# Output projection of a hybrid decoder block by seven half-size products, with operand sums by accumulating transfers

## Chip, cores and metric

One core of one Trainium2 chip. The metric is the device time of one execution in microseconds; the kernel before has a median of 1336.53 us over 3 runs (1336.42 to 1337.27).

## What is computed

One decoder block on `x` of 1024 positions by 1024 columns, all in float32:

```python
h = rmsnorm(x, mix_norm_g)
p = h @ w_in                                   # q, k, v, latents, two gates g_a and g_b
A = sliding-window attention with sinks        # window 128
B = multi-head latent attention                # causal
y = sigmoid(g_a) * (A @ w_o_swa) + sigmoid(g_b) * (B @ w_o_mla)
x = x + y @ w_out                              # the output projection: 1024 x 1024 x 1024
x = x + (silu(h2 @ w_gate) * (h2 @ w_up)) @ w_down        # h2 = rmsnorm(x), the FFN
return rmsnorm(x, final_norm_g)
```

The change concerns `x + y @ w_out` and what stands around it.

## The kernel before

**Three passes for one float32 product.** An operand is split into a high part (a cast to fp32r on ACT, L163) and a low part (the difference, on DVE, L166): this pair is what `split` makes. `mm3` (L168 to L174) multiplies two split operands by three matmuls of 128x128 by 128x512 that add up in one PSUM bank: high by high (L172), high by low (L173), low by high (L174).

**Storage.** SBUF is cut into 21 slots `U` of 4 KB and 17 slots `V` of 8 KB for each partition; a tile waits until a slot is free. PSUM has two groups of four banks: `P1` (pool `ps1`) and `PX` (in this stage pool `psc`).

**The stages in order.** Input projections; sliding-window attention (about 132 to 315 us in the profile), in whose iterations the gate projections are made too; latent attention; then the mixing of the two attentions. In `mix_a` and `mix_b` each of eight column groups `dc` gets its two gates `ga`, `gb` (tiles `sg`), on which ACT applies the sigmoid (L1277). POOL multiplies the first attention's part (tile `ar`) into `ga` (L1442, two 128x512 instructions per group: the "gate products"). TensorE makes the second attention's part `oB`, DVE multiplies it by `gb` (L1428) and adds the two (L180): that is `y`, transposed, with 128 columns of `y` on the partitions and 1024 positions along them. It is split at once into four operand pairs (`yh`, `yl`), one for each half of columns and half of positions.

**The output projection.** `xo` is made in four segments (two halves of positions by two halves of output columns) of four blocks of 128 positions. Each block is 8 k-tiles x 3 passes = 24 matmuls into one `P1` bank, and DVE adds it to the block of `x` (L180, `x<-xo,x`). `w_out` is loaded in units of 512 KB on SP's queue and split just ahead of its use; the first column half is loaded and split twice, so there are 12 units.

**Towards the FFN.** When a block of `x` is complete, ACT squares it (L1652), POOL makes the reciprocal root (L311, L314: `ms`, `rstd`), DVE scales it (L1657, `xn`), and TensorE transposes it (`to_h`, L1483, eight transposes into two `PX` banks `tp`). The FFN's products already use seven half-size products instead of eight (class `Seven`), so `to_h` also makes sums of blocks: for positions 0 to 511 it keeps copies `hraw` and splits `b11` and `b21`; for 512 to 1023 it makes `t2`, `t3`, `b22` at once, and `hraw` becomes what `t1` and `t4` are split from later (`late_split`). What `to_h` returns (`lower`, `rest`) is the second half of this work, which the code places.

**What sets the order.** Ahead of the last segment of the projection a scheduler orders the instructions of each engine. From there on (`in_order`) TensorE, DVE, ACT and POOL run in the order in which the code is written, until the FFN is under way. Each engine works its queue strictly in order, and so do SP's queue of transfers and their waits.

## Time and profile before

| | |
|---|---|
| median of 3 runs | 1336.53 us |
| the profiled execution | 1336.93 us, of which the profile's span is 1335.1 us |
| TensorE busy | 1323.6 us (99%) |
| DVE, ACT, POOL busy | 904.6, 636.5, 567.0 us |
| the projection on TensorE | 603.9 to 696.3 us, the FFN from 697.1 us |
| transfers | 223.61 MB, mean 167 GB/s, nearly all started by SP |

Busy shares are means over the whole span; the stages differ. A row of the timeline gives the start, the duration, the engine, the line and what the instruction writes and reads; in brackets stands for how long the engine had been idle and what ended that.

### The profile page before, as it was taken

The page shows a single profiled execution, that of the slowest core. Times are in us where ns is not written, and L with a number is a line of the kernel's source. Part 1 is how long each engine was busy: PE and PEld are TensorE (multiplying, and loading weights), DVE is VectorE, ACT ScalarE, POOL GpSimd, SP SyncE. Part 2 cuts the span into 40 slices and gives each one's busy share as a digit, 9 for nine tenths or more (in the row PEclk, how much of TensorE's full clock was granted, in tenths as well). Part 3 has the DMA queues.
Part 4 walks back from the last instruction along what each step waited for, and adds up shares of the span by engine and source line. Part 5 has one row for each costly group of instructions (what it writes and reads, how often), then busy time and mean ns, then how long its engine had stood idle before and what let it go on. Part 6 is the DMA issues. An engine that isn't in the chain of part 4 may idle for free. (4 is left out here: it accounts for less than half of the span.)

```text
span 1335.1 us, 19045 instructions
## 1 busy us (share of the span) xinstructions
PE 1323.6 (99%) x6564; PEld 1115.3 (84%) x6564; DVE 904.6 (68%) x1471; ACT 636.5 (48%) x1291; POOL 567.0 (42%) x614
## 2 busy tenths in 40 slices
PE   9999999999999999999999999999999999999997
PEld 6899888888888889888887888888888888888886
DVE  7868777776767767696469766666665654664862
ACT  7434676675556766753335323322233233644443
POOL 2115556552325554451131765755666541022521
PEclk9999999999999999999999999999999999999999
DMA  9454322335575530681532354534443425996504
GB/s 376 154 188 163 108 104 83 119 115 193 160 246 151 111 95 17 252 291 56 222 129 91 143 182 172 200 133 181 181 162 142 169 95 191 386 381 223 174 16 142
DMA packets 85311, 223.61 MB, mean 167 GB/s; under 512 B 9632, under 2 KB 16288, under 8 KB 84128
## 3 DMA queue, kind: packets, MB, share of 16 engines
q1 hardware_dynamic: 83776, 220.05, 47.1%
q10 hardware_dynamic: 1440, 2.36, 0.5%
q8 instruction: 52, 0.85, 0.3%
q14 instruction: 43, 0.35, 0.1%
HBM read 151.72 MB, written 70.12 MB: 166 GB/s over the span
## 5 line engine op out<-in xcount | busy, mean ns | idle before, releaser
L166 DVE TENSOR_TENSOR wl<-wr,wl 128x512 fp32r<-128x512 f32 x150 | 148.7, 1015 | 71.2 <-ACT wl L163 70.9
L166 DVE TENSOR_TENSOR lrv<-lr,lrv 128x1024 fp32r<-128x1024 f32 x77 | 105.1, 1396 | 49.0 <-ACT lrv L163 46.4
L163 ACT CAST lrv<-lr 128x1024 fp32r<-128x1024 f32 x77 | 80.1, 1052 | 95.6 <-PE fd L174 69.5
L172 PE MATMUL fd<-lrv 128*128 128x512 f32 x308 | 119.8, 389 | 0.0
L173 PE MATMUL fd<-lrv 128*128 128x512 f32 x308 | 119.8, 389 | 0.0
L174 PE MATMUL fd<-lrv 128*128 128x512 f32 x308 | 119.8, 389 | 0.0
L177 POOL TENSOR_TENSOR wr<-wr,sm 128x512 f32<-128x512 f32 (+1 forms) x38 | 45.8, 1213 | 162.6 <-DVE wl L166 136.2
L163 ACT CAST wl<-wr 128x512 fp32r<-128x512 f32 x150 | 87.0, 623 | 1.4 <-DVE wr L835 1.1
L1206 POOL TENSOR_TENSOR denb<-denb,neg_one 128x1 f32<-128x1 f32 x64 | 40.1, 627 | 96.2 <-ACT p L1205 84.4
L166 DVE TENSOR_TENSOR wl<-sm,wl 128x512 fp32r<-128x512 f32 x60 | 48.2, 829 | 42.2 <-ACT wl L163 42.1
L173 PEld LDWEIGHTS fd<-lrv 128*128 128x128 f32 x308 | 57.8, 188 | 12.1
L174 PEld LDWEIGHTS fd<-lrv 128*128 128x128 f32 x308 | 57.8, 188 | 12.0
L172 PEld LDWEIGHTS fd<-lrv 128*128 128x128 f32 x308 | 57.8, 188 | 11.9
L311 POOL TENSOR_SCALAR ms<-ss 128x1 f32<-128x1 f32 x32 | 8.9, 277 | 138.0 <-ACT xn L1652 61.1
L1205 ACT ACTIVATE p<-scb,nmb 128x384 f32<-128x384 f32 (+3 forms) x64 | 47.8, 747 | 33.3 <-DVE nmb L1204 25.6
L166 DVE TENSOR_TENSOR ptl<-pTb,pth 128x512 fp32r<-128x512 f32 (+2 forms) x96 | 50.5, 551 | 16.6 <-ACT pth L163 16.2
L1204 DVE CUSTOM_DVE_ANT_0 scb<-scb,mask 128x384 f32<-128x384 f32 (+3 forms) x64 | 48.5, 760 | 15.0 <-PE scb L1196 13.0
L1537 ACT ACTIVATE act<-sm 128x512 f32<-128x512 f32 x11 | 7.0, 632 | 104.4 <-DVE sm L180 104.4
L1207 POOL TENSOR_SCALAR p<-p,denb 128x384 f32<-128x384 f32 (+3 forms) x64 | 48.0, 749 | 6.3
L1537 ACT ACTIVATE act<-pu 128x512 f32<-128x512 f32 x22 | 13.9, 633 | 70.6 <-DVE pu L180 70.6
L163 ACT CAST pth<-pTb 128x512 fp32r<-128x512 f32 (+2 forms) x96 | 43.5, 482 | 8.5 <-PE pTb L1221 7.5
L172 PE MATMUL fb<-t2h,wl 128*128 128x512 f32 x120 | 47.4, 395 | 0.0
(356 smaller groups left out, 4319.1 us busy)
## 6 DMA issues: line engine op xcount, KB each, us to landing
lr<-la_d SPq DMA_DIRECT2D x77, 256.0 KB, 5.4
wr<-in_w_gate_dram SPq DMA_DIRECT2D x22, 512.0 KB, 4.2
wr<-in_w_up_dram SPq DMA_DIRECT2D x22, 512.0 KB, 5.0
wd<-in_w_down_dram SPq DMA_DIRECT2D x22, 512.0 KB, 6.9
rb_d<-wd SPq DMA_DIRECT2D x22, 512.0 KB, 2.7
la_d<-sd SPq DMA_DIRECT2D x22, 512.0 KB, 5.7
lr<-rb_d SPq DMA_DIRECT2D x44, 256.0 KB, 5.4
lr<-in_w_down_dram SPq DMA_DIRECT2D x33, 256.0 KB, 5.4
```

Source lines behind the costliest of these rows:

```text
L163: i = nc.scalar.copy(hi, src)
L166: (eng or nc.vector).tensor_tensor(lo, src, hi.bitcast(F32), op=ALU.subtract)
L172: nc.tensor.matmul(ps, ah, bh, start=first and i == 0, stop=False, skip_group_check=go_on)
L173: nc.tensor.matmul(ps, ah, bl, start=False, stop=False, skip_group_check=go_on)
L174: nc.tensor.matmul(ps, al, bh, start=False, stop=last and i == n - 1, skip_group_check=go_on)
L177: eng.tensor_tensor(out, a, b, op=ALU.subtract)
L311: nc.gpsimd.tensor_scalar(ms, ss, 1.0 / width, EPS, op0=ALU.mult, op1=ALU.add)
L1204: nc.vector.tensor_tensor_reduce(s_, s_, m_, 1.0, -NEG, op0=ALU.add, op1=ALU.min, accum_out=nm)
L1205: nc.scalar.activation(p_, s_, AF.Exp, scale=-1.0, bias=nm, accum_out=den)
L1206: nc.gpsimd.tensor_tensor(den, den, neg_one[:, 0:1], op=ALU.pow)
L1207: nc.gpsimd.tensor_scalar(p[:, 0:w], p[:, 0:w], den, 0.0, op0=ALU.mult, op1=ALU.add)
L1537: nc.scalar.activation(dst, src, AF.Silu)
```

## The change

**The projection as seven products.** With `y` cut into quarters (columns 0 to 511: `a`, 512 to 1023: `b`, each with positions `lo` and `hi`; `b` is kept negated) and `w_out` into `b11`, `b12`, `b21`, `b22`, seven products numbered 1, 2, 5, 6, 3, 7, 4 replace the eight. Each has four blocks of 4 k-tiles x 3 passes, 48 matmuls. Products 1, 6, 7, 4 add up in one bank per block (group `PX`), 2, 5, 3 in another (`P1`), and after each product DVE adds the bank to a half of `x` or subtracts it. That makes 28 such instructions of 128x512, before 16.

**Sums of `w_out`.** Four sums `t1` to `t4` of 1 MB are made in DRAM (`wt_d`) during the sliding-window attention: SP copies, and POOL starts transfers that add the second term to what stands there (`out_sums`, in iterations 0 to 10). 14 units are loaded and split, before 12.

**Sums of `y`.** Products 1, 2 and 4 take quarters as they are; 12 of these splits are made while mixing, where 16 were. Products 5, 7, 6 and 3 take sums, which POOL makes in place by 16 accumulating transfers between SBUF tiles, 256 KB each (`left_sum`), four for each k. The second and third of a k need the first to have landed, the third needs the second, the fourth the third. 16 more splits follow (`split_left`).

**FFN.** The subtraction that made `hraw`'s second half on DVE (4 times, 128x512) becomes an accumulating transfer on POOL (`rest`), with the sign taken into the splits of `t4`. Transposes of blocks 0 to 3 use `P1` banks, those of blocks 4 to 7 the `PX` banks of products 4, so that block 4 takes those of `xo` blocks 0 and 1, block 5 those of blocks 2 and 3, and so on in turn.

**Order.** The whole projection is now in the order of the code; the column groups are mixed in the order 0, 1, 4, 5, 2, 3, 6, 7 (before 4, 5, 0, 1, 6, 7, 2, 3), and the halves that are spilled to DRAM and read back (`ar_d`) are those of groups 4 to 7. TensorE's order at the end of the projection is: product 3 block 3, 7 block 1, transposes 2, 4 block 0, 7 block 2, transposes 3, 4 block 1, 7 block 3, transposes 4, 4 block 2, 4 block 3, transposes 5, FFN product, transposes 6, FFN product, transposes 7.

```diff
-    OUT0 = (2, 0, 3, 1)
-    for r, hf in enumerate((0, 1, 0)):
-        for j in (range(4) if r else OUT0):
-            plain(("out", r, j), w_out[hf, j], (P, 2, 512), (r, j) != (2, 3))
+    for dp in (0, 2, 1, 3):
+        plain(("ob", dp), w_o_mla[dp], (P, 4, 256), True)
+    wt_d = [dram.tile([2, P, 2, 512], F32, name=f"wt_d{i}") for i in range(4)]
+    W_SRC = {1: w_out[0, 0:2], 2: w_out[0, 2:4], 3: w_out[1, 2:4], 5: wt_d[0], 6: wt_d[1], 7: wt_d[2], 4: wt_d[3]}
+
+    def out_unit(q, u):
+        def load():
+            raw = U("wr", F32, (P, 2, 512))
+            nc.sync.dma_start(raw, W_SRC[q][u])
+            return raw
+
+        def conv(raw):
+            hi, lo = halves_of((P, 2, 512), True)
+            if q == 6:
+                a = nc.scalar.activation(hi, raw, AF.Copy, scale=-1.0)
+                nc.vector.scalar_tensor_tensor(lo, raw, -1.0, hi.bitcast(F32), op0=ALU.mult, op1=ALU.subtract)
+            else:
+                split(hi, lo, raw)
+            return hi, lo
+
+        st.add(("out", q, u), load, conv)
+
+    for q in (1, 2, 5, 6, 3, 7, 4):
+        for u in range(2):
+            out_unit(q, u)
+
+    def more(dst, src, **kw):
+        nc.gpsimd.dma_start(dst, src, accum_op=ALU.add, **kw)
+
+    def rows(t):
+        return t.rearrange("j p k c -> (j p) (k c)")
+
+    def out_sums(i):
+        b11, b12, b21, b22 = (rows(w_out[hf, 2 * kh:2 * kh + 2]) for kh in range(2) for hf in range(2))
+        t1, t2, t3, t4 = (rows(t) for t in wt_d)
+        if i == 0:
+            nc.sync.dma_start(t1, b11)
+            nc.sync.dma_start(t3, b22)
+        if i == 2:
+            more(t1, b12, max_dma_last_dim=4096)
+            more(t3, b12, max_dma_last_dim=4096)
+        if i == 4:
+            nc.sync.dma_start(t2, t1)
+        if i == 6:
+            more(t2, b22, max_dma_last_dim=4096)
+        if i == 8:
+            nc.sync.dma_start(t4, t2)
+        if i == 10:
+            more(t4, b21, max_dma_last_dim=4096)
 
 
...
@@ -1035,6 +1078,7 @@
         if it + 1 < N_SW:
             sw_qT(it + 1)
         sw[it].pop("norm")()
+        out_sums(it - 1)
         gate_step()
         if it >= 1:
...
+    left = {}
+    ya = {}
+
+    def new_left(q):
+        left[q] = (V("yh", F32R), V("yl", F32R))
+
+        ya[dc] = ga
+
+        def mixed(sh):
+            cs = half(sh)
+            if dc < 4:
+                add(ga[:, cs], ga[:, cs], gb[:, cs], nc.vector)
+            else:
+                nc.vector.scalar_tensor_tensor(ga[:, cs], ga[:, cs], -1.0, gb[:, cs], op0=ALU.mult, op1=ALU.subtract)
+            if dc >= 4 or sh == 0:
+                hi, lo = left[1 if dc < 4 else 2 if sh == 0 else 4]
+                split(hi[:, dc % 4], lo[:, dc % 4], ga[:, cs])
+
         for sh in range(2):
             cs = half(sh)
             pb = PX("oB")
             mm3(pb, [((w[0][:, c, blk(dc % 2)], w[1][:, c, blk(dc % 2)]), obT[(c, sh)]) for c in range(4)])
             nc.vector.tensor_tensor(gb[:, cs], pb, gb[:, cs], op=ALU.mult)
             if i == 7:
-                add(ga[:, cs], ga[:, cs], gb[:, cs], nc.vector)
-                split(*hT(dc, cs), ga[:, cs])
+                mixed(sh)
         for sh in range(2 if i < 7 else 0):
-            cs = half(sh)
-            add(ga[:, cs], ga[:, cs], gb[:, cs], nc.vector)
-            split(*hT(dc, cs), ga[:, cs])
+            mixed(sh)
+    def left_sum(n, *ks):
+        for k in ks:
+            a_lo, a_hi, b_lo, b_hi = (ya[k + d][:, half(sh)] for d in (0, 4) for sh in range(2))
+            more(*{0: (b_hi, a_hi), 1: (a_hi, a_lo), 2: (a_lo, b_hi), 3: (b_lo, a_lo)}[n])
+
+    def split_left(q, *ks):
+        if q not in left:
+            new_left(q)
+        d, sh = {5: (4, 1), 7: (0, 1), 6: (0, 0), 3: (4, 0)}[q]
+        for k in ks:
+            split(left[q][0][:, k], left[q][1][:, k], ya[k + d][:, half(sh)])
...
+    new_left(1)
+    SUMS = {6: [(0, 0), (0, 1)], 7: [(0, 2), (1, 0), (1, 1)]}
+    pool_order = tc.manual_schedule(engines={engines.Pool})
+    pool_order.__enter__()
+    x2 = {}
+        for n, k in SUMS.get(i, ()):
+            left_sum(n, k)
+        if i == 2:
+            new_left(2)
+            new_left(4)
         mix_b(dc, i)
...
-            ps = PX("tp", (P, 4, P))
+            ps = (P1 if b < 4 else PX)("tp", (P, 4, P))
...
-                nc.scalar.copy(raw1[b][:, kh], pss[kh])
+                nc.scalar.activation(raw1[b][:, kh], pss[kh], AF.Copy, scale=1.0 - 2 * kh)
...
-        sub(r[:, 1], r[:, 1], t23[:, 0], nc.vector)
         def rest():
+            more(r[:, 1], t23[:, 0])
             sub(t23[:, 1], pss[1], t23[:, 1], nc.vector)
...
-            split_h(name, c, r[:, i])
+            if i == 0:
+                split_h(name, c, r[:, i])
+            else:
+                hi, lo = (t[:, :, blk(c)] for t in hq[name])
+                nc.scalar.activation(hi, r[:, i], AF.Copy, scale=-1.0)
+                nc.vector.scalar_tensor_tensor(lo, r[:, i], -1.0, hi.bitcast(F32), op0=ALU.mult, op1=ALU.subtract)
...
+    def xo(q, b):
+        if q in (1, 2, 5):
+            bank[("B" if q == 1 else "A", b)] = (PX if q == 1 else P1)("xo")
+        ps = bank[("B" if q in (1, 6, 7, 4) else "A", b)]
+        w = [st.get(("out", q, u)) for u in range(2)] if b == 0 else wop[q]
+        wop[q] = w
+        lh, ll = left[q]
+        mm3(ps, [((lh[:, k, blk(b)], ll[:, k, blk(b)]), (w[k // 2][0][:, k % 2], w[k // 2][1][:, k % 2]))
+                 for k in range(4)], first=q in (1, 2, 5), go_on=q in (6, 7, 4, 3))
+        x_ = x2[b if q in (1, 2, 6, 3) else 4 + b][:, lo if q in (1, 2, 4) else hi]
+        if q in (1, 5, 7):
+            add(x_, ps, x_, nc.vector)
+        else:
+            sub(x_, x_, ps, nc.vector)
+        if b == 3:
+            left.pop(q)
+            wop.pop(q)
...
+    def norm_a(b):
+        xn = U("xn")
+        ss = tiny("ss")
+        nc.scalar.activation(xn, x2[b], AF.Square, accum_out=ss)
+        normed[b] = xn, rstd_of(ss, D)
...
-    prev = None
-    for seg, (sh, hf) in enumerate(((0, 0), (0, 1), (1, 1), (1, 0))):
...
-            else:
-                ps = P1("xo")
-                mm3(ps, [(hT(k, blk(b)), (wo2[k // 2][0][:, k % 2], wo2[k // 2][1][:, k % 2])) for k in DCS])
-            add(x2[b][:, hs], ps, x2[b][:, hs], nc.vector)
...
+    in_order.__enter__()
+    for b in range(4):
+        x2[b] = load_x(b)
+    ahead(5, 1)
+    for n, k in ((0, 3), (1, 2), (2, 0), (2, 1), (1, 3), (2, 2), (3, 0), (3, 1), (2, 3), (3, 2), (3, 3)):
+        left_sum(n, k)
+    xo(1, 0)
+    conv(5, 0)
+    xo(1, 1)
+    conv(5, 1)
+    ahead(6, 1)
+    xo(1, 2)
+    split_left(5, 0, 1)
+    xo(1, 3)
+    split_left(5, 2)
+    xo(2, 0)
+    split_left(5, 3)
+    x2[4] = load_x(4)
+    x2[5] = load_x(5)
+    xo(2, 1)
+    conv(6, 0)
+    x2[6] = load_x(6)
+    x2[7] = load_x(7)
+    xo(2, 2)
+    conv(6, 1)
+    ahead(3, 1)
+    xo(2, 3)
+    split_left(6, 0, 1)
+    xo(5, 0)
+    conv(3, 0)
+    xo(5, 1)
+    split_left(6, 2, 3)
+    xo(5, 2)
+    conv(3, 1)
+    split_left(7, 0)
+    ahead(7, 1)
+    xo(5, 3)
+    split_left(3, 0, 1)
+    split_left(7, 1)
+    xo(6, 0)
+    split_left(3, 2, 3)
+    split_left(7, 2)
+    xo(6, 1)
+    conv(7, 0)
+    split_left(7, 3)
+    xo(3, 0)
+    norm_a(0)
+    conv(7, 1)
+    ahead(4, 1)
+    ffn.load_part(0, 0)
+    xo(6, 2)
+    norm_b(0)
+    ffn.load_part(0, 1)
+    xo(3, 1)
+    norm_a(1)
+    xo(6, 3)
+    norm_b(1)
+    to_h_of(0)
+    xo(3, 2)
+    norm_a(2)
+    conv(4, 0)
+    xo(7, 0)
+    norm_b(2)
+    to_h_of(1)
+    xo(3, 3)
+    norm_a(3)
+    conv(4, 1)
+    ffn.mix(0)
+    xo(7, 1)
+    norm_b(3)
+    to_h_of(2)
+    xo(4, 0)
+    norm_a(4)
+    ffn.prep_to(1)
+    xo(7, 2)
+    norm_b(4)
+    to_h_of(3)
+    xo(4, 1)
+    norm_a(5)
+    ffn.prep_to(2)
+    xo(7, 3)
+    norm_b(5)
+    to_h_of(4)
+    xo(4, 2)
+    norm_a(6)
+    ffn.prep_to(3)
+    xo(4, 3)
+    norm_b(6)
+    norm_a(7)
+    to_h_of(5)
+    for kh in range(2):
+        ffn.load_part(1, kh)
+    norm_b(7)
     ffn.n_ahead = 1
     ffn.run()
-    late_parts.pop(0)()
+    lowers.pop(4)()
+    ffn.prep_to(4)
+    to_h_of(6)
     ffn.run()
+    lowers.pop(5)()
     ffn.prep_to(5)
-    late_parts.pop(0)()
+    to_h_of(7)
     ffn.run()
     ffn.prep_to(6)
-    lower = to_h(*prev)
-    ffn.run()
+    lowers.pop(6)()
     ffn.run()
     ffn.prep_to(7)
-    lower()
+    ffn.run()
+    lowers.pop(7)()
     ffn.prep_to(8)
```

The first place is POOL's queue at the end of the mixing. Before: the last gate products (`sg<-ar,sg`), then the first block's reciprocal root.

```order
L1442 TENSOR_TENSOR sg_6821<-ar_6825,sg_6821 128x512 x2
L1442 TENSOR_TENSOR sg_6870<-ar_6874,sg_6870 128x512 x2
L311 TENSOR_SCALAR ms_7160<-ss_7158 128x1
L314 TENSOR_TENSOR rstd_7162<-ms_7160,neg_half 128x1
L311 TENSOR_SCALAR ms_7195<-ss_7193 128x1
```

After: behind the last gate products stand the accumulating transfers. `sg_6623`, `sg_6681`, `sg_6825`, `sg_6872` hold `y` of groups 4 to 7, `sg_6470`, `sg_6603`, `sg_6730`, `sg_6778` that of groups 0 to 3. The first row of them is sum (0, k = 0), the sixth is (0, k = 3).

```order
L1513 TENSOR_TENSOR sg_6825<-ar_6829,sg_6825 128x512 x2
L1513 TENSOR_TENSOR sg_6872<-ar_6876,sg_6872 128x512 x2
L328 DMA sg_6623<-sg_6470 128x512
L328 DMA sg_6681<-sg_6603 128x512
L328 DMA sg_6825<-sg_6730 128x512
L328 DMA sg_6470<-sg_6470 128x512
L328 DMA sg_6603<-sg_6603 128x512
L328 DMA sg_6872<-sg_6778 128x512
L328 DMA sg_6730<-sg_6730 128x512
L328 DMA sg_6470<-sg_6623 128x512
L328 DMA sg_6603<-sg_6681 128x512
L328 DMA sg_6778<-sg_6778 128x512
```

All sixteen transfers stand between the last gate product and the first root.

The second place is ACT's queue at the same time. Before: the two sigmoids of the last group (`sg_6870`, `sg_6872`) stand behind the first cast of the group before it (`sg_6821`).

```order
L163 CAST wv_6992<-wr_6868 128x1024
L163 CAST yh_6609<-sg_6821 128x512
L1277 ACTIVATE sg_6870<-sg_6870 128x1024
L1277 ACTIVATE sg_6872<-sg_6872 128x1024
L163 CAST yh_6611<-sg_6821 128x512
L163 CAST yh_6609<-sg_6870 128x512
```

After: those of the last group (`sg_6872`, `sg_6874`) stand ahead of all casts of the group before it (`sg_6825`).

```order
L163 CAST yh_6619<-sg_6778 128x512
L163 CAST wv_6997<-wr_6870 128x1024
L1321 ACTIVATE sg_6872<-sg_6872 128x1024
L1321 ACTIVATE sg_6874<-sg_6874 128x1024
L163 CAST yh_6738<-sg_6825 128x512
L163 CAST yh_6740<-sg_6825 128x512
L163 CAST yh_6738<-sg_6872 128x512
```

So the sigmoid for which the last gate product waits no longer stands behind a cast that waits for DVE's sum of that group.

The third place is where the projection ends and the FFN begins. DVE before, from `xn` of block 5 (`x<-xo,x` is the projection's evacuation, `hraw`, `t`, `t2l`, `b22l`, `t3l` are the work of `to_h` on transposes `tp`):

```order
L1657 SCALAR_TENSOR_TENSOR xn_7553<-x_7380,rstd_7558,ffng_6995 128x1024
L177 TENSOR_TENSOR t_1419_7576<-tp_7565,t_1419_7576 128x512
L177 TENSOR_TENSOR t2l_7573<-t_1419_7576,t2h_7572 128x4x128
L177 TENSOR_TENSOR b22l_7571<-tp_7565,b22h_7570 128x4x128
L177 TENSOR_TENSOR t3l_7575<-t_1419_7576,t3h_7574 128x4x128
L180 TENSOR_TENSOR x_7413<-xo_7590,x_7413 128x512
L177 TENSOR_TENSOR hraw_7265<-tp_7623,hraw_7265 128x512
L177 TENSOR_TENSOR t_1427_7633<-tp_7628,hraw_7265 128x512
L177 TENSOR_TENSOR hraw_7265<-hraw_7265,t_1427_7633 128x512
L1657 SCALAR_TENSOR_TENSOR xn_7616<-x_7413,rstd_7621,ffng_6995 128x1024
L166 TENSOR_TENSOR wl_7640<-wr_7328,wl_7640 128x512
L166 TENSOR_TENSOR wl_7643<-wr_7329,wl_7643 128x512
```

DVE after, from the evacuation of product 4, block 2 (`x_7139`), with the FFN operand's split `wl_7661` behind it and the evacuation of block 3 (`x_7141`) behind that:

```order
L177 TENSOR_TENSOR x_7139<-x_7139,xo_7066 128x512
L166 TENSOR_TENSOR wl_7661<-wr_7349,wl_7661 128x512
L177 TENSOR_TENSOR x_7141<-x_7141,xo_7086 128x512
L1733 SCALAR_TENSOR_TENSOR xn_7654<-x_7139,rstd_7659,ffng_7001 128x1024
L177 TENSOR_TENSOR hraw_7457<-tp_7686,hraw_7457 128x512
L177 TENSOR_TENSOR t_1436_7696<-tp_7691,hraw_7457 128x512
L1733 SCALAR_TENSOR_TENSOR xn_7679<-x_7141,rstd_7684,ffng_7001 128x1024
L177 TENSOR_TENSOR t_1424_7636<-tp_7625,t_1424_7636 128x512
L177 TENSOR_TENSOR t2l_7633<-t_1424_7636,t2h_7632 128x4x128
L177 TENSOR_TENSOR b22l_7631<-tp_7625,b22h_7630 128x4x128
L177 TENSOR_TENSOR t3l_7635<-t_1424_7636,t3h_7634 128x4x128
L166 TENSOR_TENSOR wl_7731<-wr_7350,wl_7731 128x512
```

ACT after, at the same place (`xn_7654` is the square of block 6, `wl_7661` the cast that the split on DVE waits for):

```order
L1579 COPY t_1424_7636<-tp_7620 128x512
L1581 CAST t2h_7632<-t_1424_7636 128x4x128
L1728 ACTIVATE xn_7654,ss_7655<-x_7139 128x1024
L163 CAST wl_7661<-wr_7349 128x512
L1728 ACTIVATE xn_7679,ss_7680<-x_7141 128x1024
L1579 COPY t_1436_7696<-tp_7686 128x512
L1581 CAST t2h_7632<-t_1436_7696 128x4x128
```

The evacuation of the last block now stands behind an FFN operand, and the lower parts of blocks 4 and 5 follow when both blocks' upper parts and two `xn` are done.

103 lines of the change are left out of this document (34 added, 69 removed).

## Prediction

> **What bounds the kernel now.** I read the page first, then the waits of TensorE, the groups that touch the output projection's result `xo`, and the timelines around it.
>
> ```profile
> PE 1323.6 (99%) x6564; PEld 1115.3 (84%) x6564; DVE 904.6 (68%) x1471; ACT 636.5 (48%) x1291; POOL 567.0 (42%) x614
> ```
>
> ```profile
> PE warm L510 <- DVE warm L507: 1.2, 1, 1.2
> PE scb L1194 <- ACT p L1205: 1.1, 3, 0.6
> ...
> PE fa L172 <- ACT wl L163: 0.4, 1, 0.4
> ```
>
> TensorE is busy for 1323.6 of 1335.1 us, and its longest single wait is 1.2 us. So a matmul taken away anywhere is worth its whole spacing, provided that nothing makes TensorE wait in its place. The groups of `xo` give the number of matmuls, and TensorE's timeline their spacing:
>
> ```profile
> L172 PE MATMUL xo<-wv,yh x120: 389/389/478, 603.9 to 695.7; 128*128 128x512 f32 x120
> L173 PE MATMUL xo<-wv,yh x120: 389/389/395, 604.1 to 695.9; 128*128 128x512 f32 x120
> L174 PE MATMUL xo<-wv,yl x120: 389/389/398, 604.3 to 696.1; 128*128 128x512 f32 x120
> L180 DVE TENSOR_TENSOR x<-xo,x x16: 680/692/693, 615.4 to 697.5; 128x512 f32<-128x512 f32 x16
> ...
> L172 PE MATMUL xo<-wh,yh x8: 389/389/389, 675.5 to 694.3; 128*128 128x512 f32 x8
> ```
>
> ```profile
> 690.02 1.03 PE L1483 MATMUL tp<-ident,xn 128*128 128x128 f32 x8
> 690.81 0.48 PE L172 MATMUL xo<-wv,yh 128*128 128x512 f32 x1
> ...
> 696.35 1.04 PE L1483 MATMUL tp<-ident,xn 128*128 128x128 f32 x8
> 697.14 0.48 PE L172 MATMUL fa<-b11h,wl 128*128 128x512 f32 x1
> ```
>
> There are 3 x 120 + 3 x 8 = 384 matmuls. A group of eight transposes holds TensorE for 0.79 us (690.02 to 690.81). From 603.87 to 696.35 stand the 384 and six such groups: (92.48 - 6 x 0.79) / 384 = 0.2285 us each, with no gap worth naming. The other engines by stage (columns: TensorE, its weight loads, DVE, ACT, POOL, granted clock, DMA share):
>
> ```profile
> 132.00:315.00 183.00, 183.00 (x961) 154.97 (x961) 137.12 (x338) 125.47 (x350) 101.96 (x158) 1.00 0.32 109
> 604.00:614.10 10.10, 10.10 (x47) 8.35 (x46) 9.13 (x12) 3.87 (x7) 3.44 (x2) 1.00 0.10 41
> ...
> 624.40:634.60 10.20, 10.20 (x47) 8.45 (x46) 3.02 (x4) 1.15 (x2) 0.74 (x2) 1.00 0.13 51
> 696.30:720.00 23.70, 23.13 (x107) 18.36 (x106) 20.84 (x31) 14.61 (x27) 4.05 (x4) 1.00 0.37 131
> ```
>
> ```profile
> 604.00:696.30 92.30, 92.30 (x433) 76.87 (x432) 50.81 (x63) 32.86 (x54) 18.10 (x22) 1.00 0.32 122
> ```
>
> The clock is full, so nothing is to be had from it. DVE enters the projection nearly saturated (9.13 of 10.10 us), has room in the middle (3.02 of 10.20) and is nearly saturated again when the FFN begins (20.84 of 23.70). POOL (0.74 of 10.20) and the DMA engines (0.13) are almost empty in the middle. That is where the change puts its sums, and the two full places of DVE are where it can lose what it gains.
>
> **The gain.** Seven products of 4 blocks x 4 k x 3 passes are 336 matmuls, 48 fewer: 48 x 0.2285 = **-11.0 us**. FFN would begin at 603.87 + 336 x 0.2285 + 6 x 0.79 = 685.4 instead of 697.1; 0.8 of that difference is the seventh transpose group, which now stands behind the FFN's first product and is no gain.
>
> **The left-hand sums.** Sixteen accumulating transfers of 256 KB go out on POOL behind its last gate product. No row shows an accumulating transfer, or any that POOL starts. The nearest rows:
>
> ```profile
> gate_d<-go SPq DMA_DIRECT2D x32, 256.0 KB, 2.1
> wr<-in_w_out_dram SPq DMA_DIRECT2D x12, 512.0 KB, 6.9
> xt<-in_x_t_dram SPq DMA_DIRECT2D x7, 512.0 KB, 9.6
> ```
>
> ```profile
> 612.58 0.68 DVE L1428 TENSOR_TENSOR sg<-oB,sg 128x512 f32<-128x512 f32 x1
> ```
>
> ```profile
> 606.64 3.44 POOL L1442 TENSOR_TENSOR sg<-ar,sg 128x512 f32<-128x512 f32 x2 [4.71 <-ACT sg L1277]
> 633.24 0.19 POOL L311 TENSOR_SCALAR ms<-ss 128x1 f32<-128x1 f32 x1 [23.16 <-ACT xn L1652]
> ```
>
> The lower end is 2.1 us, the upper 9.6. The quiet 256 KB store is nearest (DMA share 0.10 to 0.13 here), but an accumulate reads two operands, so I take **4 us** from issue to landing, and 1.2 us of POOL per issue, a choice between the 0.2 and 1.7 us of POOL's rows here (one 128x1 operation, one gate product). Call the 4 us L. The last gate product ended at 610.1 because its sigmoid on ACT stood behind a cast that waited for DVE; in the new order it stands ahead of it, so POOL is free some 6 us earlier, at about 604 (at 610 the chain below ends 6 us later and still holds). The order on POOL then makes a chain of five landings: sum (0,0); (1,0), which waits for it, with (1,1) and (0,3) behind it in POOL's order; then (1,3), (2,3), (3,3). (What (0,3) adds is ready on DVE at about the same time: the last multiplication, at 612.58, comes four splits of 0.60 earlier, 610.2, and one addition follows.) The last lands at about 604.2 + 2.4 + 5 L = 606.6 + 5 L: near 627 to 629 for L = 4. It is needed for the third block of sums in product 3, whose first block runs from 642.2 and meets k = 3 at 644.3, less 1.3 us for a cast and a split: 643. The slack is 14 us, and it breaks at L = 7. So the sums cost nothing here; beyond 6.5 us every further microsecond of L costs five, since the splits also stand ahead of evacuations in DVE's order.
>
> [...]
>
> **The right-hand sums.** Four 1 MB copies on SP and four accumulates on POOL fall between 132 and 315 us. DMA is 0.32 busy there, at 109 GB/s, 20 MB in all; 8 MB more raise it to near 0.5. What waits behind them: on POOL the softmax divisions and gate mixing, on SP the gate-weight loads.
>
> ```profile
> POOL den L937 <- ACT pe L933: 52.2, 14, 7.0
> ```
>
> POOL sits idle 52 us there waiting for ACT, in pieces of up to 7 us, which covers an issue of a few us. Bounds: 0 and 4 x 2.4 (twice the rows, twice 1.2) = 10 us if none were covered; I take 0.
>
> **DVE's added work.** 12 splits and 12 evacuations more of 128x512, 2 operand splits of 128x1024, and 4 subtractions fewer: 20 x 0.60 + 2 x 1.2 = 14.4 us, by the spacing of the rows below (0.60 us from one 128x512 to the next, whose 0.68 overlap; 1.2 us for a 128x1024). Between 604 and 696.3 DVE was busy for 50.81 us; 65 fit into the 81 us that are left, on average. The places where it doesn't are the last three bank reuses, at the end of the projection:
>
> ```profile
> 684.72 1.06 ACT L1652 ACTIVATE xn<-x 128x1024 f32<-128x1024 f32 x1 [4.30 <-DVE x L180]
> 685.69 0.18 ACT L1652 ACTIVATION_READ_ACCUMULATOR xn<-x 128x1 f32 x1
> ...
> 693.84 1.66 ACT L163 CAST wl<-wr 128x512 fp32r<-128x512 f32 x3
> ```
>
> ```profile
> 687.13 1.28 DVE L1657 SCALAR_TENSOR_TENSOR xn<-x,rstd,ffng 128x1024 f32<-128x1024 f32 x1 [0.45 <-POOL rstd L314]
> 688.34 0.68 DVE L177 TENSOR_TENSOR t<-tp,t 128x512 f32<-128x512 f32 x1
> 688.94 0.68 DVE L177 TENSOR_TENSOR t2l<-t,t2h 128x512 fp32r<-128x512 f32 x1
> 689.73 0.69 DVE L177 TENSOR_TENSOR b22l<-tp,b22h 128x512 fp32r<-128x512 f32 x1
> ```
>
> (a) Transposes of block 5 need the banks of product 4, blocks 2 and 3. Between the two evacuations DVE now splits an FFN operand, whose cast stands on ACT behind the square of block 6, which needs the first evacuation. From the end of block 2: 0.2 + 0.7 (evacuation) + 1.2 (square) + 0.5 (cast) + 0.7 (split) + 0.7 (evacuation) + 0.3 for handing over = 4.3; TensorE has 12 x 0.2285 = 2.7 to do: 1.6 us, and 2.7 with DVE one subtraction late. I take 2.3. (b) Transposes of block 6 need block 4's banks, free only after DVE's xn, 2 subtractions, xn, t, t2l, b22l: 2 x 1.2 + 5 x 0.62 = 5.5, and 0.4 for the hand-over; TensorE has 0.8 + 2.7: 2.3 us. (c) Transposes of block 7 need the same of block 5: from the start of block 6's transposes 1.1 + 0.7 + 0.7 (two subtractions) + 3 x 0.65 (t, t2l, b22l) + 0.6 (ACT's cast of b22) = 5.1 against 3.5: 1.6 us. Together **+6.2**. In the old kernel this stretch has 23.70 - 23.13 = 0.57 us of such waits, which go.
>
> The wide cast and split of product 4's second operand also stand behind a square, but six matmuls run before they are needed: +0.3, at most 2. Product 1 shares banks with `oB`, the last of which DVE multiplied at 612.58, 8.7 us after `xo` had begun. The new order puts these multiplications ahead of all sums, so I cost it at 0; if DVE stays as late as it was, block 1 waits some 2 us. The operand loads (14 of 512 KB, 12 before) wait for fewer free slots; their cover is the 11 us of a product against 6.9 us to land, so 0.
>
> Sum: -11.0 + 6.2 - 0.6 + 0.3 = **-5.1 us**. The profiled execution took 1336.93 us, 0.4 above the median: 1331.8 there, 1331.4 against the median of 1336.53.
>
> **Rivals.** *No wait appears* (10%): DVE finds its operands earlier than I place them, and the gain stays whole: -11.0, 1325.5. For it: (a) to (c) come out of a queue worked by hand. Against it: DVE's 20.84 of 23.70.
>
> *DVE and POOL slow each other* (15%, no change). The timeline shows what stands beside POOL's work:
>
> ```profile
> 604.21 0.68 DVE L180 TENSOR_TENSOR sg<-sg,sg 128x512 f32<-128x512 f32 x1
> ...
> 607.14 1.77 DVE L180 TENSOR_TENSOR sg<-sg,sg 128x512 f32<-128x512 f32 x1
> ```
>
> The same addition takes 0.68 us alone and 1.77 beside the last gate product (606.64 to 610.08). If the transfers did a little of this for longer, so that DVE's spacing were 0.70 instead of 0.60, then the 45 or so instructions that DVE runs from 640 to the transposes of block 5, where it has nothing to spare, add 0.1 us each: some 4 us more, -1, 1335.5. [...]
>
> *The chain of sums becomes the bound* (25%, slower). Decided at L: at 8 us the last sum lands at 646.6, 3.6 after its time; with the operations behind it in DVE's order some 9 us of waits in products 6 and 3 and the first transposes, so -5.1 + 9 = +4, 1340.5. At the upper row's 9.6 it is +12, 1348.5. An issue of 2.5 us instead of 1.2 does nearly the same (16 issues, 20 us more on POOL, 8 of waits: +3). From L = 7.5 it is no longer a gain. For it: five landings in a row, unlike anything in this trace; against it: idle DMA engines and 14 us of slack.
>
> *The change doesn't do what it says*: excluded, as the new order has 48 fewer `xo` rows on TensorE.
>
> **Chances.** Forecast 50% (1328 to 1334), no wait 10%, DVE drag 15%, chain 25%. A measurement here can tell 0.2% (2.7 us) from no change. Faster by more: 0.60; within: 0.15; slower: 0.25. The range takes in the case with no wait and the chain up to L = 9: 1325.5 to 1345.5.
>
> **What will show it.** `xo` has 336 matmuls at 0.2285 us; FFN's first matmul starts near 688. Waits of TensorE before the transposes of blocks 5, 6 and 7 are each about 2 us on DVE. Every sum lands in 3 to 6 us, the last before 640, and no `xo` matmul waits for a cast of a sum. It is wrong if TensorE waits in products 5, 6 or 3 for ACT's `yh` casts, if POOL is held more than 2 us per issue, or if TensorE waits anywhere from 132 to 315 us.

## The result and the profile after

| | before | after |
|---|---|---|
| median | 1336.90 us (6 runs, 1336.09 to 1338.10) | 1341.57 us (6 runs, 1339.97 to 1344.19) |
| profiled execution, its span | 1336.93, 1335.1 us | 1341.21, 1339.4 us |

The ratio is 1.0034 [1.0023, 1.0044]: the changed kernel is slower by some 4.6 us. The forecast was 5.1 us faster; the time lies in the range, on the other side. The 48 matmuls did go. First the page's busy times, then the groups of `xo`, after:

```profile
PE 1320.3 (99%) x6516; PEld 1108.3 (83%) x6516; DVE 921.7 (69%) x1493; ACT 644.3 (48%) x1305; POOL 586.9 (44%) x638
```

```profile
L172 PE MATMUL xo<-wv,yh x112: 389/389/632, 610.3 to 695.2; 128*128 128x512 f32 x112
L173 PE MATMUL xo<-wv,yh x112: 387/389/632, 610.5 to 695.5; 128*128 128x512 f32 x112
L174 PE MATMUL xo<-wv,yl x112: 388/389/632, 610.8 to 695.7; 128*128 128x512 f32 x112
```

There are 3 x 112 = 336, and yet TensorE is busy for only 3.3 us less, not 11.0. The third number of a group is its longest instruction: 632 ns, where before none was above 478. And the projection begins 6.4 us later (610.3, before 603.9). So time was lost ahead of it too. TensorE's waits, after (total, times, longest):

```profile
PE tp L1562 <- ACT t L1579: 2.4, 2, 1.8
PE oB L172 <- DVE sg L1490: 2.1, 1, 2.1
PE xo L173 <- DVE wv L166: 1.8, 1, 1.8
...
PE xo L174 <- DVE yl L166: 0.4, 1, 0.4
PE fa L174 <- DVE wl L166: 0.4, 2, 0.3
PE fa L172 <- ACT pu L855: 0.4, 2, 0.2
```

Three waits of about 2 us are new: one in the mixing (`oB`), one in the projection (`xo`), one at the transposes (`tp`). Where the time went is best read from the first instruction of each stage in TensorE's timeline, since no wait can hide between two such points:

| stretch on TensorE | before | after | more | forecast |
|---|---|---|---|---|
| start to the last transpose of the sliding-window stage | 313.29 | 315.40 | +2.1 | 0 |
| from there to the first `oB` | 247.06 | 247.03 | 0 | 0 |
| first `oB` to first `xo` (mixing) | 43.52 | 47.87 | +4.35 | 0 |
| first `xo` to first FFN product (`fa`) | 93.27 | 86.42 | -6.85 | -9.2 |
| first `fa` to first `fb` | 24.24 | 28.95 | +4.7 | +4.1 |
| behind that | | | 0 | 0 |

(The last two forecasts sort the terms of the sum: of -11.0 + 6.2 - 0.6 + 0.3 the first wait (a) and the +0.3 belong to the projection; the seventh group of transposes, 0.8 us, moves from one row to the next.) The rows add up to +4.3, as the profiled executions do. The forecast is off by 9.4: 2.1, 4.35, 2.35 and 0.6.

**The mixing.** TensorE's timeline after, around the wait:

```profile
603.08 0.50 PE L172 MATMUL oB<-obT,wv 128*128 128x512 f32 x1 [2.11 <-DVE sg L1490]
...
604.12 0.63 PE L173 MATMUL oB<-obT,wv 128*128 128x512 f32 x1
...
607.10 0.58 PE L174 MATMUL oB<-obT,wv 128*128 128x512 f32 x1
607.52 0.40 PE L172 MATMUL oB<-obT,wv 128*128 128x512 f32 x1
```

and DVE's, of the few microseconds ahead of it:

```profile
596.09 1.21 DVE L166 TENSOR_TENSOR wv<-wr,wv 128x1024 fp32r<-128x1024 f32 x1
...
598.42 1.77 DVE L180 TENSOR_TENSOR sg<-sg,sg 128x512 f32<-128x512 f32 x1
600.12 2.30 DVE L166 TENSOR_TENSOR wv<-wr,wv 128x1024 fp32r<-128x1024 f32 x1
602.34 0.68 DVE L1490 TENSOR_TENSOR sg<-oB,sg 128x512 f32<-128x512 f32 x1
```

A product of `oB` waits for a bank that DVE frees at 602.34, and ahead of that stands the split of an operand of product 2. It takes 2.30 us, where a split of the same size took 1.21 at 596.09: a gate product of POOL begins at 599.61. Then a second loss follows that no wait shows: about 1 us after TensorE resumes, eight matmuls start 0.43 us apart instead of 0.23 (604.12 to 607.10), 1.6 us more. Two stretches of the profile, one ahead of this loss and one over it, give the clock (the columns are as in the prediction):

```profile
600.66:604.08 3.42, 1.31 (x6) 0.86 (x5) 2.96 (x3) 0.00 (x0) 0.68 (x1) 1.00 0.71 175
604.08:607.49 3.41, 3.41 (x9) 2.67 (x8) 3.27 (x6) 3.23 (x4) 0.63 (x1) 0.50 0.89 310
```

The granted clock of the second stretch is half, and TensorE still counts as wholly busy in it. In all 16 matmuls ran so in this execution, here and once more in the projection: 3.1 us that the busy time holds and no wait shows.

**The projection.** The wait in it, on ACT and on DVE, after:

```profile
673.23 1.06 ACT L1728 ACTIVATE xn<-x 128x1024 f32<-128x1024 f32 x1 [3.08 <-DVE x L177]
...
674.28 1.03 ACT L163 CAST wv<-wr 128x1024 fp32r<-128x1024 f32 x1
```

```profile
675.35 2.26 DVE L166 TENSOR_TENSOR wv<-wr,wv 128x1024 fp32r<-128x1024 f32 x1 [2.29 <-ACT wv L163]
```

ACT stands idle for 3.08 us in front of a square that waits for DVE's evacuation; behind it stands the cast of product 4's second operand, and behind that DVE's split, which again takes twice its time (POOL works on FFN weight sums from 675.25). TensorE waits 1.79 us at 677.66, and eight matmuls at half clock follow here too.

**The sums.** Transfers, after, in the window 604 to 650:

```profile
q0 software_dynamic: 2304, 4.20, 50.9%
q1 hardware_dynamic: 1570, 5.71, 38.6%
...
sg<-sg POOLq DMA_DIRECT2D x16, 256.0 KB, 6.5
```

and POOL's timeline:

```profile
606.86 3.34 POOL L1513 TENSOR_TENSOR sg<-ar,sg 128x512 f32<-128x512 f32 x2 [5.52 <-ACT sg L1321]
610.14 1.85 POOL L328 DMA_DIRECT2D sg<-sg  x2
613.83 0.85 POOL L328 DMA_DIRECT2D sg<-sg  x1 [1.84 <-DVE yl L166]
...
643.82 0.87 POOL L328 DMA_DIRECT2D sg<-sg  x1 [1.73 <-DMA sg<-sg]
```

The sums begin at 610, not at 604, since the last gate product still waits 5.5 us for its sigmoid. ACT's timeline has the cast two places ahead of that sigmoid:

```profile
604.25 0.62 ACT L163 CAST yh<-sg 128x512 fp32r<-128x512 f32 x1 [5.47 <-DVE sg L180]
```

So the sigmoid does still stand behind a cast that waits for a sum of DVE's, that of another group than before, and DVE is late there at least in part for the reason above: with product 2's splits out of the mixing (below) the sums begin at 606.5. An issue holds POOL for 0.87 us. From issue to landing it is 3.3 us at the least, 6.5 in the middle and 8.1 at the most. The DMA engines, 0.11 busy in this window before, are 0.90 busy now, over half of it with 4.2 MB of sums. The last sum goes out at 643.82, and TensorE waits for a split of it once, 0.44 us.

### The profile page after: what moved, and what is told of

Same layout as the page of the kernel before. It is cut to its first block, busy times and chain, and to the rows that moved or that the text cites. A ratio compares the mean times of both kernels' runs of the same rounds, so it can differ in the third digit from the quotient of the medians.

```text
span 1339.4 us, 19065 instructions
## 1 busy us (share of the span) xinstructions
PE 1320.3 (99%) x6516; PEld 1108.3 (83%) x6516; DVE 921.7 (69%) x1493; ACT 644.3 (48%) x1305; POOL 586.9 (44%) x638
## 5 line engine op out<-in xcount | busy, mean ns | idle before, releaser
L166 DVE TENSOR_TENSOR wl<-wr,wl 128x512 fp32r<-128x512 f32 x150 | 153.3, 1044 | 80.3 <-ACT wl L163 79.9
```

Of the source, the lines that this page charges most:

```text
L166: (eng or nc.vector).tensor_tensor(lo, src, hi.bitcast(F32), op=ALU.subtract)
```

## Experiments

The theory after this profile: the loss is in the places that I had costed at nothing. Two wide splits stand badly on DVE and each costs a wait and, here, a stretch at half clock; the sums themselves cost little. The rival: the sums, by filling the DMA engines and holding POOL, are the cause, and the waits are only where they show. Ratios are to the kernel before (1337.4 to 1337.8 us in these runs).

**Without the right-hand sums.** Products 5, 6, 7 and 4 read plain quarters of the weight, so their results are not the block's.

```diff
-    W_SRC = {..., 5: wt_d[0], 6: wt_d[1], 7: wt_d[2], 4: wt_d[3]}
+    W_SRC = {..., 5: w_out[0, 0:2], 6: w_out[0, 2:4], 7: w_out[1, 0:2], 4: w_out[1, 2:4]}
-        out_sums(it - 1)
```

> The four right-hand sums are left out (products 5, 6, 7 and 4 take plain quarters of w_out instead, so the output isn't the block's): no copies and no accumulating transfers from 132 to 315 us. Ledger theory: TensorE arrives at the end of that stage 2.1 us late because the second 1 MB accumulate holds POOL for 7.7 us, so without them the transposes pT at 192 us don't wait and the whole run is 2.1 us shorter: 1339.5 us, ratio to before 1.0018. Rival (DVE is the bound behind it and eats whatever arrives earlier): the stage is 2.1 us shorter, the run by under 0.7 us. Second rival (the copies on SP are what costs): the same 2.1 us here, told apart by the run that only spreads the accumulates.

Measured: 1340.62 us, 1.0022 [1.0013, 1.0031]. The sliding-window stage ends at 314.59 (after 315.40, before 313.29). The size fits 1 to 2 us, but one interval overlaps the other, and this stage alone ends anywhere from 314.4 to 317.9, at 315.7 in the mean, in the eleven profiles that kept these sums. By itself this run decides nothing; the last one of this study bears on it again.

**The right-hand sums spread out.** In the changed kernel POOL stands still between the first and the second sum of 1 MB:

```profile
184.41 0.92 POOL L328 DMA_DIRECT2D wt_d<-in_w_out_dram x1 [7.70 <-issue]
```

The first was issued at 175.60, and nothing else stands between them. Here the second goes out one iteration later. If it stands still only while the first is under way, the hold goes; if a sum of 1 MB holds POOL by itself, it moves along:

```diff
             more(t1, b12, max_dma_last_dim=4096)
+        if i == 3:
             more(t3, b12, max_dma_last_dim=4096)
```

> The second of the two 1 MB accumulates that POOL issues in one iteration moves to the next iteration, nothing else. [...] Rival (an accumulate of 1 MB holds POOL that long by itself, or waits for its copy): the hold of 7 us moves with it to the next iteration, and the time stays at 1341.6.

POOL's timeline of this kernel has no idle time ahead of either issue:

```profile
176.89 1.10 POOL L328 DMA_DIRECT2D wt_d<-in_w_out_dram  x1
188.69 0.95 POOL L328 DMA_DIRECT2D wt_d<-in_w_out_dram  x1
```

Measured: 1343.09 us, 1.0029 [1.0016, 1.0042]. The hold of 7.7 us is gone; the time can't be told from the changed kernel's. So that hold costs TensorE little, and what these sums cost is not this one wait. What the second sum waits for in the changed kernel no row names.

**Product 2's wide splits moved behind the start of the projection.**

```diff
-        if i >= 4:
-            st.conv_to(st.index[("out", 1 + i // 6, i % 2)])
+        if 4 <= i < 6:
+            st.conv_to(st.index[("out", 1, i % 2)])
...
     xo(1, 0)
-    conv(5, 0)
+    conv(2, 0)
     xo(1, 1)
-    conv(5, 1)
-    ahead(6, 1)
+    conv(2, 1)
     xo(1, 2)
+    conv(5, 0)
     split_left(5, 0, 1)
     xo(1, 3)
+    conv(5, 1)
+    ahead(6, 1)
```

> DVE's two wide splits of product 2's operands leave the mixing stage and stand behind product 1's first two evacuations. Ledger theory: the 12th multiplication by a gate ends about 2 us earlier, TensorE's wait of 2.1 us in oB at 603 us goes, and with it the half-speed matmuls that followed it (1.7 us): the run is 3.5 to 4 us shorter, 1337.6 us, ratio 1.0005, and no oB matmul takes 0.63 us. Rival (DVE is the bound of the whole projection): the wait in oB goes, but the two splits delay the evacuations of products 1 and 2 and the sums' splits, waits of 2 to 4 us appear in products 2 or 5, and the run is within 1 us of 1341.6.

Its waits:

```profile
PE xo L173 <- DVE wv L166: 2.0, 2, 1.8
...
PE tp L1562 <- DVE x L177: 0.8, 1, 0.8
PE xo L174 <- DVE yl L166: 0.8, 1, 0.8
PE tp L1562 <- DVE xn L1733: 0.7, 1, 0.7
```

The row of `oB` is gone, and the mixing takes 44.44 us, 3.4 less than after. The place is right. Measured: 1341.33 us, 1.0025 [1.0016, 1.0034], less than expected, and the interval overlaps the changed kernel's: the times alone show no gain. 1.3 us came back as waits at the transposes of blocks 4 and 6 (the two rows of 0.8 and 0.7), where the changed kernel had 0 and 0.2. The profiled execution took 1338.57 us, the fastest of the eleven, so where the median's time went is not shown.

**Product 4's cast ahead of the square.**

```diff
-    norm_a(2)
     conv(4, 0)
+    norm_a(2)
...
-    norm_a(3)
     conv(4, 1)
+    norm_a(3)
```

> ACT casts product 4's operands ahead of the squares of blocks 2 and 3 instead of behind them, nothing else. Ledger theory: the wait of 1.8 us at product 4's first block (it and its hand-over 2.1) and the half-speed matmuls behind it (1.6) go: 3 to 3.7 us shorter, 1338.2 us, ratio 1.001. Rival (DVE's throughput at the end is what counts): the same time is waited for at the transposes of blocks 5 to 7, under 1 us is left of the gain, 1341 us.

In this kernel the split comes earlier, and beside no multiplication of POOL:

```profile
670.45 1.22 DVE L166 TENSOR_TENSOR wv<-wr,wv 128x1024 fp32r<-128x1024 f32 x1
```

TensorE's timeline of this kernel, around the wait in the mixing:

```profile
602.86 0.50 PE L172 MATMUL oB<-obT,wv 128*128 128x512 f32 x1 [2.10 <-DVE sg L1490]
...
604.12 0.39 PE L174 MATMUL oB<-obT,wv 128*128 128x512 f32 x1
```

Measured: 1339.10 us, 1.0009 [1.0000, 1.0018], as expected. Product 4's wait is gone. TensorE's rows show something else: the wait in the mixing is as long as it was, 2.10 us, but no half clock follows it, though the edit touches nothing there. In the profile the projection is 2.2 us shorter, 0.6 us came back behind it, and 1.7 us are this half clock that did not come; so the number agrees partly by luck.

**The left-hand sums left out.** The sixteen accumulating transfers are dropped and the splits read plain quarters of `y`, so the result is not the block's.

```diff
-            more(*{0: (b_hi, a_hi), 1: (a_hi, a_lo), 2: (a_lo, b_hi), 3: (b_lo, a_lo)}[n])
+            pass
```

> The sixteen accumulating transfers of y are left out; the splits behind them read the plain quarters, so the output isn't the block's. Ledger theory: the sums cost only the wait of about 0.7 us at product 3's first block, so 0.7 to 1 us shorter, 1340.7 us, ratio 1.0028; the waits in oB, at product 4 and at the last transposes stay as they are. Rival (the prediction's own: the chain of sums, at 6.5 us each, is what made the kernel slower): 5 us or more shorter, at or below the time before.

Measured: 1339.05 us, 1.0011 [1.0002, 1.0020], between the two. By the medians these sums cost 0.0023, 3 us. The wait in the mixing stays (2.1, with no half clock after it), that for product 4 is halved (0.9, with none either). So the sums are a part of it and not the cause.

**The gate products left out.** POOL's two multiplications per column group are dropped, so the sliding-window part of `y` lacks its gate.

```diff
-            nc.gpsimd.tensor_tensor(gate[dc][:, half(sh)], a_[:, half(sh)], gate[dc][:, half(sh)], op=ALU.mult)
+            pass
```

> POOL's sixteen gate products are left out (y lacks their factor, so the output isn't the block's). If DVE falls behind in the mixing because its splits of 128x1024 run beside POOL's gate products (2.3 us each instead of 1.2, four times), then without them these splits take 1.2 us, DVE is 3 to 4 us earlier at the 11th multiplication, the wait in oB at 603 us goes, and POOL starts the sums some 6 us earlier: 4 to 5 us shorter, 1337 us, ratio 1.000. Rival (DVE is late because of the order in which casts and splits of y now follow each other, not because of POOL): the wait in oB stays above 1.5 us, and at most 1 us is gained.

DVE's timeline of this kernel, the last wide split of the mixing and the multiplication behind it:

```profile
597.07 1.22 DVE L166 TENSOR_TENSOR wv<-wr,wv 128x1024 fp32r<-128x1024 f32 x1
598.21 0.69 DVE L1490 TENSOR_TENSOR sg<-oB,sg 128x512 f32<-128x512 f32 x1
```

Measured: 1336.05 us, 0.9986 [0.9978, 0.9995], faster than expected. All seven wide splits of the mixing take 1.2 us, no product of `oB` waits, and the mixing takes 43.52 us, as before the change. That POOL's multiplications are what lengthens the split, from 1.22 to 2.30 us, is shown. The projection is 2.75 us shorter besides: product 4 waits 0.8 us, and no half clock follows. The kernel before has these multiplications too, so its time isn't one that the change could reach in this way.

**The transposes one product later.** Transposes 6 and 7 each go behind one more FFN product, and the lower parts of blocks 5 and 7 ahead.

```diff
     lowers.pop(4)()
     ffn.prep_to(4)
-    to_h_of(6)
-    ffn.run()
     lowers.pop(5)()
+    ffn.run()
+    to_h_of(6)
     ffn.prep_to(5)
-    to_h_of(7)
     ffn.run()
+    to_h_of(7)
...
     ffn.prep_to(7)
+    lowers.pop(7)()
     ffn.run()
-    lowers.pop(7)()
```

> The transposes of blocks 6 and 7 each stand one FFN product later on TensorE, and the lower half of block 5 ahead of block 6's upper half on DVE; nothing else. Ledger theory: the waits of 0.2, 0.6 and 1.8 us at these transposes are covered by a product of 2.7 us each: 2.5 us shorter, 1339.1 us, ratio 1.0015. Rival (DVE is behind by that much anyway): the wait moves to the FFN's first fb product, whose operands come from block 7, and under 0.7 us is left.

Its waits:

```profile
PE fa L174 <- DVE wl L166: 2.3, 1, 2.3
...
PE fa L172 <- ACT pu L855: 2.0, 1, 2.0
...
PE tp L1562 <- DVE b22l L177: 1.7, 1, 1.7
```

Measured: 1345.86 us, 1.0069 [1.0053, 1.0085]. This theory fell. The waits for `t` went, but the FFN operand, the evacuation of the FFN product and `b22l` now stand behind the moved work, and TensorE waits 6 us for them. In the changed kernel DVE is busy for 20.63 of the 25 us from 697 on, and this order only changed what TensorE waits for.

**The four subtractions back on DVE** (`hraw`'s second half, with the sign taken out of the splits of `t4`):

```diff
+        sub(r[:, 1], r[:, 1], t23[:, 0], nc.vector)
...
-            more(r[:, 1], t23[:, 0])
```

> The kernel after with one part undone: the four subtractions for t4 are back on DVE, no accumulating transfers towards the FFN. Theory (DVE is late only by its waits there): each adds 0.6 us on DVE between the upper parts of blocks 4 to 7, of which about 1.5 us reach the last transposes: 1 to 2 us slower than the kernel after, ratio 1.004 to 1.005. [...]

Measured: 1343.94 us, 1.0043 [1.0030, 1.0057], as expected. By the medians this part of the change saves some 1 us, though the intervals overlap.

**The two good moves together**, then with the transposes' order of above, then instead with the FFN casts ahead of the squares:

```diff
-    norm_a(4)
     ffn.prep_to(1)
+    norm_a(4)
```

(the same for blocks 5 and 6)

> The two moves that removed their wait when made alone (product 2's splits behind the mixing; product 4's casts ahead of the squares), without the one on the last transposes, with the whole computation. Theory (the waits are separate, each with its own place): 1.2 to 2.5 us from the first, 3.3 from the second, so 1336.5 to 1337 us, ratio 0.9995 to 1.000. Rival (DVE is the bound of the stretch and its lateness is handed on): no more than the second move alone, ratio 1.0009.

> The three moves together (product 2's splits behind the mixing, product 4's casts ahead of the squares, the last transposes one product later), with the whole computation. Ledger theory: the savings add, 1.2 to 4 + 3.3 + 2.5 us, so 1332 to 1334.5 us, ratio 0.9965 to 0.998, below the kernel before: the 48 matmuls were worth their 11 us, and their gain had gone into these waits. Rival (DVE as the bound of the stretch): what one move saves the next loses, 1337.5 us or more, ratio 1.000 or more.

> As the two moves together, and ACT casts the FFN's first three operands ahead of the squares of blocks 4, 5 and 6 too, so that DVE doesn't stand still 1.8 us three times ahead of the evacuations behind their splits. Theory (the waits at the last transposes come from ACT's order, as the prediction's step (a) had it): DVE is nearly 2 us earlier there, the waits at the transposes of blocks 5 to 7 fall from 3.3 us to about 1, ratio 0.998 to 0.999. Rival (they come from the chain hraw, copy, t2, b22 through both engines, whatever is ahead): within 0.5 us of the two moves.

Measured: both moves 1337.20 us, 0.9999 [0.9990, 1.0007]; with the transposes' order 1343.20 us, 1.0039 [1.0026, 1.0051], spoilt by the same three waits as alone; with the casts first 1336.13 us, 0.9990 [0.9980, 1.0000]. That is by its median the fastest kernel here that leaves nothing out, and no more than level with the kernel before. The waits at the transposes fell from 3.4 us (both moves) to 2.3, not to the 1 that was expected, and the intervals of the two kernels overlap, so the casts' part isn't shown by the time. Waits of TensorE, casts first:

```profile
PE tp L1562 <- ACT t L1579: 2.1, 2, 1.8
...
PE xo L174 <- DVE yl L166: 0.7, 1, 0.7
PE xo L172 <- ACT yh L163: 0.7, 1, 0.7
```

The waits for `oB` and for product 4 are gone and no matmul runs at half clock, and still most of the 11 us is missing. The last run asks where the rest is.

**Casts first, with all sums and gate products left out** (the three edits of above in one; the result is not the block's, but the 336 matmuls and the order stay).

> The kernel with both moves and the FFN casts ahead of the squares (1336.1 us, 0.999), and besides it leaves out three parts of the computation: the sixteen left-hand sums (their splits read plain quarters of y), the right-hand sums (products 5, 6, 7 and 4 read plain quarters of the weight), and POOL's gate products in the mixing. So it keeps the 336 matmuls, and leaves only what the changed order of the casts, splits and transposes costs by itself. Theory: the costs found so far lie at different places and add up. By the trace of the kernel with casts first, the two waits of 0.8 and 0.9 us for splits of summed operands (643 and 650 us) and the small gaps of 0.4 and 0.2 at 618 and 620 go, and 1 us of the sliding-window stage: 1336.1 - 2.3 - 1.0 = 1332.8 us, ratio 0.9965 (0.9955 to 0.9975). The waits of the end stay: about 1.8 us before the transposes of block 7, 0.4 to 0.6 before those of block 6. Rival: what bounds there is DVE and ACT's own order, so that what is taken out is waited for again behind it: 0.998 or more. If all of the 11 us came back, 1326.5 us, 0.992, neither is right, and something in the sums holds the other places too.

Measured: 1330.00 us, 0.9946 [0.9932, 0.9960], more than expected (0.9965), and far from the rival. Its longest wait from the mixing on:

```profile
PE tp L1561 <- ACT t L1578: 2.1, 2, 1.8
```

By stretches, against the kernel with casts first: the sliding-window stage ends at 313.36 instead of 315.22, where it ended before the change; the mixing takes 43.52 instead of 44.40, as before the change; the projection 81.98 instead of 85.67. 336 x 0.2285 + 6 x 0.79 is 81.5, so all but 0.5 of the 11.0 us are there. Only the stretch behind the first FFN product keeps its loss, 28.32 us against 24.24, of which 0.8 is the seventh group of transposes. So the sums and POOL's gate products together cost 6.4 us even in the best order: 1.9 in the sliding-window stage, where only the right-hand sums were taken out, 0.9 in the mixing, 3.7 in the projection, of which 1.4 are the two waits of 0.7 and the rest smaller pauses. How the mixing's and the projection's part divides between left-hand sums and gate products was not measured.

## Why the prediction was wrong

**The gain** of 11.0 us (48 matmuls at 0.2285) is right: the last run has it to 0.5 us. The steps that failed are terms that were put at nothing, or nearly, and cost time.

**The mixing** is the step that failed worst. It was put at 0, with the note that block 1 of `xo` might wait 2 us "if DVE stays as late". It cost 4.35 us. The wait came earlier than I looked, inside the mixing, and in the profiled execution 1.6 us at half clock followed its 2.1. Before, the multiplication that frees this bank started at 596.67 and the product that needs it at 598.43, a slack of about 1 us; I had not looked that up. Ahead of that product stand six wide splits of the mixing in either kernel. Beside gate products fell two of them before and four after:

```profile
596.67 0.68 DVE L1428 TENSOR_TENSOR sg<-oB,sg 128x512 f32<-128x512 f32 x1
597.27 1.21 DVE L166 TENSOR_TENSOR wv<-wr,wv 128x1024 fp32r<-128x1024 f32 x1
```

(DVE's timeline before; the second row is the split that then had its place behind the multiplication.) Taking away either the split (44.44 us) or POOL's products (43.52) makes the wait go. I had the mechanism among the rivals, priced on the 0.68 us that became 1.77, but looked for it only behind 640, where POOL multiplies nothing. The run without the gate products shows it: 1.22 us without them against 2.30 beside them.

**Product 4's second operand**, +0.3, "at most 2", cost 3.9 in the profiled execution: 2.3 of wait and pauses in the block that needs it, and 1.6 at half clock. The step named the right queue, the cast behind a square, but took the split at 1.2 us where it took 2.26, and did not see that ACT stands idle at that square.

**The left-hand sums**, put at 0, cost 3 us by the medians (1.0034 to 1.0011 without them). They don't come on top of the two steps above: a part of product 4's wait goes with them. The landing was taken at 4 us and is 6.5; POOL was taken to be free at 604 and is at 610. The 1.2 us for an issue, and the 2.5 of the rival, no run shows: an issue holds POOL for 0.87. By the prediction's own formula the last sum would land at 610 + 2.4 + 5 x 6.5 = 645; it was issued at 643.8 and landed 3.3 later. But POOL's start and L were both off, and the rival of the chain, whose 1340.5 us lies near the measured time, came near it by luck: it has 9 us of waits for sums, and the wait for the last sum is 0.44 us. "Idle DMA engines" was the wrong argument against it: with sixteen sums they are 0.90 busy.

**The right-hand sums**, put at 0, cost some 1 to 2 us: the stage ends at 315.7 in the mean of eleven profiles with them, at 314.6 and 313.4 in the two without, and at 313.3 before. The two without differ by 1.2 us though nothing up to there is different in them, so the size is rough. TensorE has no single wait there of note; what stretches the stage was not settled beyond that. The 2.4 us that the bound had for an issue no run shows: the four hold POOL for 0.92 to 1.11 us each.

**The tail** cost less than forecast, and its mechanism was wrong: 2.3, 2.3 and 1.6 us were forecast before transposes 5, 6 and 7, and the pauses are 0, 1.2 and 2.1. (The 2.7 in step (a) doesn't follow from its own numbers; 1.6 and one subtraction are the 2.3 that it took. Its 0.3 for handing over, and the 0.4 of step (b), no row shows: after the change TensorE starts 0.05 and 0.06 us behind DVE's operation, at 677.66 and 603.08.)

```profile
695.93 1.03 PE L1562 MATMUL tp<-ident,xn 128*128 128x128 f32 x8
...
699.89 0.66 PE L1562 MATMUL tp<-ident,xn 128*128 128x128 f32 x4 [0.18 <-DVE xn L1733]
701.15 0.66 PE L1562 MATMUL tp<-ident,xn 128*128 128x128 f32 x4 [0.60 <-ACT t L1579]
...
706.88 0.66 PE L1562 MATMUL tp<-ident,xn 128*128 128x128 f32 x4 [1.80 <-ACT t L1579]
```

```profile
697.96 0.68 DVE L177 TENSOR_TENSOR x<-x,xo 128x512 f32<-128x512 f32 x1
```

Step (a), like the section on the change, had transposes 5 take the banks of product 4's blocks 2 and 3. But DVE evacuates block 3 only at 697.96, when the transposes of 695.93 are done and the FFN's first product is under way. So they had another bank, and their pause is 0 in every profile of this study, also where product 4's operand is not waited for. The two waits that do come end with ACT's copy `t` (L1579), not with the `b22l` that steps (b) and (c) name. This copy empties the first of a block's two banks, well ahead of `b22l`; that a bank goes on as soon as it is emptied, instead of keeping its turn with block 3's, fits all these waits but was not tried by a run of its own.

Where product 4's delay goes, 0.4 to 0.5 us come back before transposes 4 and about 0.5 before transposes 6 (both moves: 0.4 and 1.8). The FFN's own products wait 0.8 us besides. In all 3.9 us more than before are lost behind the first `fa`, against 3.3 forecast there, and nothing at transposes 5 against 2.3.

## What to carry to other kernels

Where TensorE is 99% busy, a term of nothing has to be read as a slack: for each instruction that is moved, look up how long before its need the thing behind it finishes now, and at what duration beside POOL it will run (here 2.30 us for a split that takes 1.22 without POOL's products). Here a wait of 2.1 us had 1.6 us at half clock behind it in one execution and none in others, and a wait that went uncovered the next one: with product 2's splits moved the mixing was 3.4 us shorter, and 1.3 us came back as waits at the transposes. So single fixes gave less than their waits. Work that is moved to POOL and to transfers isn't free because they are idle: without the sixteen left-hand sums the changed kernel was 3 us faster, and without all sums and the gate products, which the kernel before has too, the best order was 6 us faster.

## What the chip showed besides

**Half clock after a short wait.** In the changed kernel's profile eight matmuls about 0.43 us apart instead of 0.23 follow two waits of TensorE: the 2.11 us in the mixing, and the 1.79 us for product 4. Each such stretch lasts 3.41 us at a granted clock of 0.50 (604.08 to 607.49 above, and this one) and loses some 1.6 us:

```profile
679.17:682.58 3.41, 3.41 (x10) 2.67 (x9) 2.46 (x4) 0.86 (x1) 3.33 (x3) 0.50 0.04 16
```

Behind the 1.80 us before transposes 7 (706.88) none follows in the same execution. Nor does the mixing's wait decide it by its length: after 2.10 us with product 4's cast first, 2.07 without the left-hand sums and 2.09 with the subtractions back on DVE the matmuls stay 0.23 us apart. With the subtractions on DVE those behind product 4's wait of 1.79 us are again 0.43 us apart, from 680.16. What decides it was not tried by a run of its own, so the 1.6 us are what an execution lost here, not a price that can be forecast from a wait.

**Accumulating transfers** of 256 KB between SBUF tiles hold POOL for 0.87 us each in the changed kernel, land after 3.3 to 8.1 us, and take the 16 DMA engines 50.9% of 46 us for 4.2 MB, 1.5 us each. Behind the 1 MB sum in DRAM issued at 175.60 the second one waits 7.7 us on POOL and goes out at 184.41; issued 12 us after the first (176.89 and 188.69, the sums spread out) it has no idle time ahead of it.
